# An expert ring of six split pairs and five raw tiles, with one-hots, splits and low parts moved

## The chip, the cores and the metric

The kernel runs on one core of a Trainium2 chip. A core has a matrix engine (TensorE; PE in the profile, its weight loads PEld), a vector engine (VectorE, DVE), a scalar engine (ScalarE, ACT), GpSimd (POOL) and a queue engine that only issues transfers (SyncE, SP). Each runs its own instructions in order and waits on semaphores for the others. Tiles live in SBUF (128 partitions); results of PE land in PSUM. The metric is the device time of one execution in microseconds, the median over runs.

## The reference

A two-layer encoder over 512 tokens of width 1024. Each layer has a mixer (differential attention in layer 0, a sparse latent attention in layer 1), attention to a memory of 256 tokens, and a hierarchical mixture of 16 experts, each followed by a residual and a layer norm. The change touches the mixture:

```python
g_sel = argmax(t @ w_group + b_group)                # 4 groups of 4 experts
top_val, top_idx = top_k(e_logits of the group, 2)   # two experts for each token
top_w = softmax(top_val) * g_gate
for e in range(16):
    hid = silu(t @ w_gate[e]) * (t @ w_up[e])        # 1024 -> 512
    y = y + combine[:, e:e+1] * (hid @ w_down[e])    # 512 -> 1024
```

All in float32. An expert's weights are three matrices of 2 MB, 6 MB together.

## The kernel before

**Split matmuls.** A product in float32 is made of three in the faster format fp32r: an operand is split into a high part (ACT copies it to fp32r, L208 for weights, L258 for activations) and a low part (DVE subtracts the high part from the raw tile, L209 and L259), and PE adds high x high, high x low and low x high.

**Units and the ring.** An expert's weights come in six units of 1 MB, 128 x 2048: j = 0, 1 (gate), 2, 3 (up), 4, 5 (down). `Stream` (object `U`) loads a unit into a raw tile (`ahead`, on SP's queue, L233), and `get` splits it into a pair of tiles (`wsplit`). The order of all 96 units of a layer is `ORDER`: for expert p the four units into the hidden layer, then the two down units of expert p-1. There are RING = 7 split pairs, from the pools `act8` (8 tiles) and `w8` (6 tiles), and RB = 3 raw tiles. `refill(n)` makes units up to n + RING: a unit's pair is free when the unit seven back has been used. Three units are split ahead of the mixture, beside the projection in front of it (NFIRST).

**Blocks.** Tokens are gathered by expert. A block is up to 128 tokens of one expert; the experts at places p = 5 and 11 (`DBL`) have a second block (v = 16, 17). For a block, `slot_rows` makes four one-hot tiles on DVE (L833 to L843, tiles pw, pv, pb, oh), `slot_sums` multiplies them on PE (L849, pi), `slot_out` makes the row numbers sx and gate weights sw (DVE, L855 and L857), and `gather` fetches the rows with an indirect DMA from POOL's queue (L870) into a tile that POOL has set to zero (L866). For experts 0 and 1, `slot_tokens` makes the row numbers in a shorter way, from one-hots in two buffers. `turn` transposes a block on PE (L877, xgT) and splits it (xh on ACT, xl on DVE).

**The loop.** For each p, in program order, which is the order on every engine here: set the tile of a later block (p+2) to zero, its one-hots on DVE; where that expert has two blocks, also their sums on PE and their gathers; `refill` of the unit left over from the round before (`late`); gate (PE, pg, then SiLU on ACT, L1071), up (pu), each unit followed by a `refill`; sums and gather of block p+2 where it is single; the product hid (DVE, L1081); `turn` of the next block, in two halves: its transposes, then the `refill` of the up projection's last unit, then xh and xl; the down projection of p-1 (py, L918, scaled on ACT, L907, and added to memory by an indirect DMA from POOL's queue, L908); transposes and split of hid (hT, hsh, hsl). At p = 0 the slots of experts 0 and 1 are computed after `turn`. The router (`router`) is a generator whose parts are issued in places: position numbers, permutation (`prm`), weights (`who, cv`), and the list of extra blocks (`xtra`, at p = 2), whose count is loaded into registers at p = 4 for a conditional part at the end.

PSUM tiles of 1024 columns (`sc2`: xgT and py among them) have two buffers, so py for an expert, or a second transpose, waits until xl has read an earlier xgT.

Of the kernel before, what the change touches and what calls it, by code (L numbers as in the profile page):

```python
# [22 lines left out]
P = 128  # L23
# [41 lines left out]
def encoder(ctx: ExitStack, tc: tile.TileContext, I, out):  # L65
# [137 lines left out]

    def wsplit(raw, hi, lo, scale=None, chunks=1):
        if scale is None:
            n = raw.shape[1] // chunks
            for c in (slice(j * n, j * n + n) for j in range(chunks)):
                nc.scalar.activation(hi[:, c], raw[:, c], AF.Copy)  # L208
                nc.vector.tensor_tensor(lo[:, c], raw[:, c], hi[:, c].bitcast(F32), op=ALU.subtract)  # L209
        else:  # L210
            for k in range(raw.shape[1]):
                nc.scalar.activation(hi[:, k], raw[:, k], AF.Copy, scale=scale(k))
                nc.vector.scalar_tensor_tensor(lo[:, k], raw[:, k], scale(k), hi[:, k].bitcast(F32),
                                               op0=ALU.mult, op1=ALU.subtract)
        return hi, lo

    class Stream:
# [4 lines left out]

        def add(self, name, src, shape=(P, 8, 256), scale=None, alloc=w8, depth=RB):
            loads = src if callable(src) else (lambda raw: [(raw, src)])
            self.units.append((name, loads, list(shape), scale, alloc, depth))

        def ahead(self, depth, q=nc.sync):
            for m in range(self.n, min(self.n + depth, len(self.units))):
                if m not in self.raw:
                    nm, loads, shape, _, alloc, _ = self.units[m]  # L230
                    self.raw[m] = r8(f"{nm}r", shape)
                    for sl, src in loads(self.raw[m]):
                        q.dma_start(sl, src)  # L233

        def get(self, name, chunks=1):
            n = self.n
            nm, _, shape, scale, alloc, depth = self.units[n]
            assert nm == name, (nm, name)
            self.ahead(1)
            W = wsplit(self.raw[n], alloc(name + "h", shape), alloc(name + "l", shape), scale, chunks)  # L240
            self.n += 1
            self.ahead(depth)
            return W

# [572 lines left out]
    def slot_tokens(pos, nm):  # L817
        o = tp(f"pi{nm}")
        for t in range(NT):
            oh = sb.tile([P, P], F16, tag="oh", name=f"oh{nm}{t}", bufs=2)  # L820
            nc.vector.tensor_scalar(oh, iota16, pos[:, t:t + 1], None, op0=ALU.is_equal)
            nc.tensor.matmul(o[:, 0:1], oh, tokm[:, t:t + 1], start=t == 0, stop=t == NT - 1)
        idx = small(f"ix{nm}", [P, 1], I32)
        last_ix[0] = nc.vector.tensor_scalar(idx, o[:, 0:1], float(NONE), None, op0=ALU.add)
        return idx

    def slot_rows(who, cv, e, base, nm):

        pw = small(f"pw{nm}", [P, NT, 8], bufs=3)
        pv = small(f"pv{nm}", [P, NT, 8], bufs=2)  # L830
# [7 lines left out]
        for t in range(NT):  # L838
            oh.append(sb.tile([P, P], BF16, tag="ohf", name=f"oh{nm}{t}", bufs=4))
            if base is None:  # L840
                nc.vector.tensor_scalar(oh[t], iotab, pw[:, t, 0:1], None, op0=ALU.is_equal)  # L841
            else:
                nc.vector.tensor_scalar(oh[t], iotab, base, pw[:, t, 0:1], op0=ALU.add, op1=ALU.is_equal)  # L843
# [86 lines left out]
    ORDER = moe_order()  # L930

    PERM, XU = {}, {}

    def moe(i, R, before, after, first):
# [12 lines left out]
        def block(j):  # L947
# [13 lines left out]
            def W(q):  # L961
                src, shape = us[q]
                hi, lo, raw = [t.rearrange("p (a b) -> p a b", a=shape[1]) for t in X + [XR]]
                nc.sync.dma_start(raw, src)
# [80 lines left out]
        with tc.manual_schedule(engines={ENG.PE, ENG.Activation, ENG.DVE}):  # L1045
            for v in range(S0):
                gather(slot_tokens(posm[:, :, v], name(v)), xg[v])
                if v == 0:
                    refill(3 - RING)
            refill(5 - RING)  # L1050
            turn(0)()
            prm, PERM[i] = next(rt)
            who, cv = next(rt)
            refill(6 - RING)
            late = None
            for p in range(NE):
                cur, nxt = blocks[p], blocks.get(p + 1, [])
                new = blocks.get(p + 2, [])
                for v in new:
                    xg[v] = gather_begin(name(v))  # L1060
                    R_[v] = rows(v)
                    if len(new) > 1:
                        SX[v] = slot_out(R_[v], slot_sums(R_[v], name(v)), name(v))
                        gather(SX[v][0], xg[v])
                if late is not None:
                    refill(late)
                refill(way_in(pg, cur, p, 0))
                n = way_in(pg, cur, p, 1)
# [8 lines left out]
                n = way_in(pu, cur, p, 3)  # L1077
                if len(new) == 1:
                    pt = slot_sums(R_[new[0]], name(new[0]))
                for v in cur:  # L1080
                    nc.vector.tensor_tensor(hid[v], hid[v], pu.pop(v), op=ALU.mult)  # L1081
# [33 lines left out]
            for n in range(2):  # L1115
                down_part(1, py, hT, W[1], (n,))
            X = [w8(f"X{i}{k}", [P, 2048]) for k in range(2)]
            XR = act8(f"XR{i}", [P, 2048], F32)
            XG = gather_begin(f"{i}_x")
# [259 lines left out]
    def plan():  # L1379
# [43 lines left out]
        for i in range(2):  # L1423
# [110 lines left out]
```

## Time and profile before

| | |
|---|---|
| median of 3 runs | 1908.26 us (1907.23 to 1912.56) |
| the profiled execution | 1901.26 us, of it the span 1899.5 us |
| mean granted clock of PE | 0.916 |
| PE busy | 1603.6 us (84%) |
| DVE busy | 1195.4 us (63%) |
| ACT busy | 853.3 us (45%) |
| POOL busy | 259.5 us (14%) |

The span is the time from the first to the last instruction that the profile shows. A row of the table of stages gives a stretch, its length, then for each engine its busy time and number of instructions, then the granted clock (1.00 is full), the mean busy share of the 16 DMA engines and what they moved in GB/s. A row of waits gives who waited for what: the total in us, how often, the longest. A row of a timeline gives start, duration, engine, line, operation, the tile written and those read, shapes, a count, and in brackets the idle time of the engine before it and what ended that. Expert loops run from about 567 to 991 us (layer 0) and from 1454 to 1875 us (layer 1).

### The profile page before, as it was taken

Reading aid. Unit: us, or ns where it says so; the run is one execution under the profiler, and the core shown is the slowest. Engines: PE = TensorE matmul, PEld = TensorE weight load, DVE = VectorE, ACT = ScalarE, POOL = GpSimd, SP = SyncE. Lnnn points to the kernel's source line nnn. Section 1 sums busy time; section 2 is a strip of 40 time slices with the busy share of each in tenths; the row PEclk is TensorE's granted clock in tenths of the full one; section 3 lists DMA queues with packets and bytes.
Section 4 is the critical chain, followed back from the end, with each engine's and each line's share of the span. In section 5 each row is a group of like instructions: output and inputs, shape, how many; then the busy total and the mean of one; then the engine's idle time right before and its main releaser. Section 6 shows DMA issues by size and latency. Waiting matters only on the chain. (4 is left out here: it accounts for less than half of the span.)

```text
span 1899.5 us, 24536 instructions
## 1 busy us (share of the span) xinstructions
PE 1603.6 (84%) x9244; PEld 1354.6 (71%) x9244; DVE 1195.4 (63%) x2317; ACT 853.3 (45%) x1142; POOL 259.5 (14%) x230
## 2 busy tenths in 40 slices
PE   7999899988957688879887889999895768868895
PEld 7887798887855577767667656898694657757773
DVE  4444546453477776777657698463358786678675
ACT  4343436232324465655543445533323555556562
POOL 1000001110040221222210000020012121232111
PEclk9999999899977799989897999999997879989998
DMA  7220325233165787887774102141516777788784
GB/s 202 67 67 1 101 95 192 92 123 113 67 234 174 236 276 236 267 270 242 252 246 142 45 23 78 54 144 51 164 47 210 253 239 239 243 271 276 239 285 135
DMA packets 122435, 317.67 MB, mean 167 GB/s; under 512 B 23773, under 2 KB 81117, under 8 KB 97728
## 3 DMA queue, kind: packets, MB, share of 16 engines
q1 hardware_dynamic: 104496, 272.00, 43.0%
q0 software_dynamic: 17808, 43.96, 7.6%
q8 instruction: 77, 1.26, 0.3%
q14 instruction: 54, 0.44, 0.1%
HBM read 299.38 MB, written 36.70 MB: 177 GB/s over the span
## 5 line engine op out<-in xcount | busy, mean ns | idle before, releaser
L870 POOL DMA_INDIRECT xg<-h_d,sx x32 | 57.7, 1804 | 422.0 <-DVE sx L857 357.9
L908 POOL DMA_INDIRECT acc_d<-y,sx x34 | 78.1, 2297 | 241.5 <-ACT y L907 211.8
L208 ACT ACTIVATE mw_1h<-mw_1r 128x2048 fp32r<-128x2048 f32 x32 | 61.4, 1917 | 108.9 <-PE pg L891 76.2
L209 DVE TENSOR_TENSOR mw_3l<-mw_3r,mw_3h 128x2048 fp32r<-128x2048 f32 x32 | 73.3, 2289 | 49.3 <-ACT mw_3h L208 49.3
L209 DVE TENSOR_TENSOR mw_2l<-mw_2r,mw_2h 128x2048 fp32r<-128x2048 f32 x32 | 73.3, 2291 | 44.1 <-ACT mw_2h L208 43.2
L209 DVE TENSOR_TENSOR mw_5l<-mw_5r,mw_5h 128x2048 fp32r<-128x2048 f32 x32 | 73.3, 2290 | 43.9 <-ACT mw_5h L208 43.6
L209 DVE TENSOR_TENSOR mw_1l<-mw_1r,mw_1h 128x2048 fp32r<-128x2048 f32 x32 | 73.3, 2289 | 35.6 <-ACT mw_1h L208 34.8
L208 ACT ACTIVATE mw_5h<-mw_5r 128x2048 fp32r<-128x2048 f32 x32 | 61.2, 1914 | 63.9 <-PE py L918 35.8
L208 ACT ACTIVATE mw_3h<-mw_3r 128x2048 fp32r<-128x2048 f32 x32 | 61.3, 1916 | 61.9 <-DMA mw_3r<-in_moe_w_up_dram 40.3
L918 PE MATMUL py<-mw_4h,hsh 128*128 128x512 f32 x144 | 63.3, 439 | 24.4 <-DVE xl L259 23.0
L209 DVE TENSOR_TENSOR mw_4l<-mw_4r,mw_4h 128x2048 fp32r<-128x2048 f32 x32 | 73.4, 2294 | 16.0 <-ACT mw_4h L208 14.9
L849 PE MATMUL pi<-pb,oh 128*128 128x6 bf16 x144 | 14.4, 175 | 81.1 <-DVE oh L841 68.8
L208 ACT ACTIVATE mw_4h<-mw_4r 128x2048 fp32r<-128x2048 f32 x32 | 61.3, 1916 | 48.0 <-DMA mw_4r<-in_moe_w_down_dram 27.9
L891 PE MATMUL pg<-mw_0h,xl 128*128 128x512 f32 x144 | 66.5, 462 | 10.4 <-DVE xl L259 10.3
L209 DVE TENSOR_TENSOR mw_0l<-mw_0r,mw_0h 128x2048 fp32r<-128x2048 f32 x32 | 73.1, 2284 | 1.7 <-ACT mw_0h L208 1.4
L849 PEld LDWEIGHTS <-oh 128*128 128x128 bf16 x144 | 8.8, 99 | 91.5 <-DVE oh L841 70.1
L891 PE MATMUL pg<-mw_0h,xh 128*128 128x512 f32 x144 | 70.0, 486 | 3.4 <-ACT xh L258 3.4
L208 ACT ACTIVATE mw_2h<-mw_2r 128x2048 fp32r<-128x2048 f32 x32 | 61.2, 1913 | 22.5 <-DMA mw_2r<-in_moe_w_up_dram 22.4
L877 PE MATMUL xgT<-ident,xg 128*128 128x128 f32 x288 | 45.3, 306 | 29.9 <-DVE xl L259 20.2
L891 PE MATMUL pg<-mw_0l,xh 128*128 128x512 f32 x144 | 65.8, 457 | 0.0
L208 ACT ACTIVATE mw_0h<-mw_0r 128x2048 fp32r<-128x2048 f32 x32 | 61.4, 1918 | 8.5 <-DMA mw_0r<-in_moe_w_gate_dram 8.5
L877 PEld LDWEIGHTS xgT<-ident,xg 128*128 128x128 f32 x288 | 38.8, 197 | 32.2 <-DVE xl L259 21.9
(944 smaller groups left out, 5653.2 us busy)
## 6 DMA issues: line engine op xcount, KB each, us to landing
mw_0r<-in_moe_w_gate_dram SPq DMA_DIRECT2D x32, 1024.0 KB, 5.5
mw_1r<-in_moe_w_gate_dram SPq DMA_DIRECT2D x32, 1024.0 KB, 6.6
mw_2r<-in_moe_w_up_dram SPq DMA_DIRECT2D x32, 1024.0 KB, 6.3
mw_3r<-in_moe_w_up_dram SPq DMA_DIRECT2D x32, 1024.0 KB, 5.9
mw_4r<-in_moe_w_down_dram SPq DMA_DIRECT2D x32, 1024.0 KB, 5.5
mw_5r<-in_moe_w_down_dram SPq DMA_DIRECT2D x32, 1024.0 KB, 5.5
mhx<-acc_d POOLq DMA_DIRECT2D x8, 512.0 KB, 6.8
x<-in_x_dram SPq DMA_DIRECT2D x4, 512.0 KB, 6.7
```

The costliest lines, as they stand in the source:

```text
L208: nc.scalar.activation(hi[:, c], raw[:, c], AF.Copy)
L209: nc.vector.tensor_tensor(lo[:, c], raw[:, c], hi[:, c].bitcast(F32), op=ALU.subtract)
L849: nc.tensor.matmul(o[:, 0:6], rows[2][t], rows[1][:, t, :], start=t == 0, stop=t == NT - 1)
L870: nc.gpsimd.indirect_dma_start(out=x, out_offset=None, in_=h_d[:, :], in_offset=bass.IndirectOffsetOnAxis(ap=idx[:, 0:1], axis=0), bounds_ ...
L877: nc.tensor.transpose(pt[:, ts(k)], x.rearrange("n (p k) -> n k p", k=8)[:, k, :], ident)
L891: nc.tensor.matmul(o, xT[l][:, a, :], W[r][:, k, :], start=a == j == 0, stop=a == 7 and j == 2)
L908: nc.gpsimd.indirect_dma_start(out=acc_d[:, :], out_offset=bass.IndirectOffsetOnAxis(ap=ix[:, 0:1], axis=0), in_=y, in_offset=None, bounds ...
L918: nc.tensor.matmul(o, hs[a][:, ts(2 * q + f)], Dq[b][:, f, c], start=q == f == k == 0, stop=q == f == 1 and k == 2)
```

## The change

- **Ring.** RING goes from 7 to 6 split pairs, and raw tiles from three to RAWS = 5. Both are now fixed tiles, kept in `Cells` for each layer: unit n uses pair n mod 6 and raw tile n mod 5; the two added raw tiles come from the pool of the pair that was given up. NFIRST goes from 3 to 2. The tiles of the conditional part at the end are taken from these cells.
- **Low parts on Pool.** `wsplit` and `get` take an engine. For the last unit of an expert (j = 5), except expert 0, the low part is a subtraction on POOL's queue.
- **One-hots lead.** In each round the one-hots of all new blocks, at p = 0 and 1 also those of block p itself, are issued first; their sums come after the up projection, and sx, sw and the gathers after hid, also for doubled experts. One-hot tiles have 8 buffers, shared with those of `slot_tokens`; `pw` has two instead of three. Single blocks compare a float16 iota plus a constant.
- **xl ahead.** `turn` of the next block is issued whole, ahead of the `refill` of the up projection's last unit.
- **Router and start.** `prm` is issued ahead of the first `turn`; refills at the start are fewer and later; `xtra` moves from p = 2 to p = 5, the load of its count from p = 4 to p = 12.

```diff
-NFIRST = 3
-RING = 7
+NFIRST = 2
+RING = 6
+RAWS = 5
...
-                nc.vector.tensor_tensor(lo[:, c], raw[:, c], hi[:, c].bitcast(F32), op=ALU.subtract)
+                eng.tensor_tensor(lo[:, c], raw[:, c], hi[:, c].bitcast(F32), op=ALU.subtract)
...
-            oh.append(sb.tile([P, P], BF16, tag="ohf", name=f"oh{nm}{t}", bufs=4))
+            oh.append(sb.tile([P, P], BF16, tag="ohf", name=f"oh{nm}{t}", bufs=8))
             if base is None:
-                nc.vector.tensor_scalar(oh[t], iotab, pw[:, t, 0:1], None, op0=ALU.is_equal)
+                nc.vector.tensor_scalar(oh[t], iota16, BIG, pw[:, t, 0:1], op0=ALU.add, op1=ALU.is_equal)
...
+    class Cells:
+        def raw(self, n):
+            def get(name, shape):
+                q = n % RAWS
+                if q < RB:
+                    t = self.tile(("r", q), lambda nm, sh, dt: r8(nm, sh), F32)
+                else:
+                    t = self.tile(("r", q), act8, F32)
+                return self.view(t, shape)
+            return get
+
+        def part(self, n):
+            k = iter("hl")
+            def get(name, shape):
+                q = n % RING
+                return self.view(self.tile((next(k), q), w8 if 1 <= q <= 3 else act8, F32R), shape)
+            return get
...
-                unit[made[0]] = U.get(f"mw{i}_{p}_{j}")
+                unit[made[0]] = U.get(f"mw{i}_{p}_{j}", eng=nc.gpsimd if j == 5 and p else nc.vector)
...
                 gather(slot_tokens(posm[:, :, v], name(v)), xg[v])
-                if v == 0:
-                    refill(3 - RING)
-            refill(5 - RING)
+                refill(2 + v - RING)
+            prm, PERM[i] = next(rt)
             turn(0)()
-            prm, PERM[i] = next(rt)
             who, cv = next(rt)
-            refill(6 - RING)
-            late = None
+            late = 5 - RING
             for p in range(NE):
                 ...
                 for v in new:
                     xg[v] = gather_begin(name(v))
+                if p < S0:
+                    new = new + [p]
+                for v in new:
                     R_[v] = rows(v)
-                    if len(new) > 1:
-                        SX[v] = slot_out(R_[v], slot_sums(R_[v], name(v)), name(v))
-                        gather(SX[v][0], xg[v])
                 ...
-                if len(new) == 1:
-                    pt = slot_sums(R_[new[0]], name(new[0]))
+                pts = {v: slot_sums(R_[v], name(v)) for v in new}
                 for v in cur:
                     nc.vector.tensor_tensor(hid[v], hid[v], pu.pop(v), op=ALU.mult)
                     xT.pop(v)
-                if len(new) == 1:
-                    v = new[0]
-                    SX[v] = slot_out(R_[v], pt, name(v))
-                    gather(SX[v][0], xg[v])
+                for v in new:
+                    SX[v] = slot_out(R_[v], pts.pop(v), name(v))
+                    if v != p:
+                        gather(SX[v][0], xg[v])
                 for v in nxt[:1]:
-                    done = turn(v)
-                    refill(n)
-                    done()
-                if p == 0:
-                    for v in range(S0):
-                        R_[v] = rows(v)
-                        SX[v] = slot_out(R_[v], slot_sums(R_[v], name(v)), name(v))
-                if p == 2:
-                    xtra = next(rt)
+                    turn(v)()
+                refill(n)
                 ...
+                if p == 5:
+                    xtra = next(rt)
                 if p + 3 == NE:
                     sel, wsel = last_select()
-                if p == 4:
+                if p == 12:
                     nx = nc.values_load(xtra["n"][0:1, 0:1], engines=IF_ENG, min_val=0, max_val=NX)
...
-                free = ORDER.index((S0, 0)) if n < RING else len(ORDER)
+                free = ORDER.index((S0, 0)) if n < 4 else len(ORDER)
                 U.add(f"mw{i}_{p}_{j}", loads, (P, 4, 512) if j < 4 else (P, 2, 1024),
-                      alloc=(act8, w8)[n % 7 % 2], depth=min(RB, free - n - 1))
+                      alloc=CELLS[i].part(n), raw=CELLS[i].raw(n), depth=min(RAWS, free - n - 1))
```

More of the change, by code (lines that the diff above doesn't have):

```diff
@@ L202, in rsqrt, with wsplit @@
         return y
-    def wsplit(raw, hi, lo, scale=None, chunks=1):
+    def wsplit(raw, hi, lo, scale=None, chunks=1, eng=nc.vector):
         if scale is None:
@@ L221, in __init__, with add @@
             self.units, self.raw, self.n = [], {}, 0
-        def add(self, name, src, shape=(P, 8, 256), scale=None, alloc=w8, depth=RB):
+        def add(self, name, src, shape=(P, 8, 256), scale=None, alloc=w8, depth=RB, raw=r8):
             loads = src if callable(src) else (lambda raw: [(raw, src)])
-            self.units.append((name, loads, list(shape), scale, alloc, depth))
+            self.units.append((name, loads, list(shape), scale, alloc, depth, raw))
         def ahead(self, depth, q=nc.sync):
@@ L229, in ahead, with get @@
                 if m not in self.raw:
-                    nm, loads, shape, _, alloc, _ = self.units[m]
-                    self.raw[m] = r8(f"{nm}r", shape)
+                    nm, loads, shape, _, _, _, raw = self.units[m]
+                    self.raw[m] = raw(f"{nm}r", shape)
                     for sl, src in loads(self.raw[m]):
                         q.dma_start(sl, src)
-        def get(self, name, chunks=1):
+        def get(self, name, chunks=1, eng=nc.vector):
             n = self.n
-            nm, _, shape, scale, alloc, depth = self.units[n]
+            nm, _, shape, scale, alloc, depth, _ = self.units[n]
             assert nm == name, (nm, name)
             self.ahead(1)
-            W = wsplit(self.raw[n], alloc(name + "h", shape), alloc(name + "l", shape), scale, chunks)
+            W = wsplit(self.raw[n], alloc(name + "h", shape), alloc(name + "l", shape), scale, chunks, eng)
             self.n += 1
@@ L819, in slot_tokens @@
         for t in range(NT):
-            oh = sb.tile([P, P], F16, tag="oh", name=f"oh{nm}{t}", bufs=2)
+            oh = sb.tile([P, P], F16, tag="ohf", name=f"oh{nm}{t}", bufs=8)
             nc.vector.tensor_scalar(oh, iota16, pos[:, t:t + 1], None, op0=ALU.is_equal)
@@ L827, in slot_rows @@
     def slot_rows(who, cv, e, base, nm):
-        pw = small(f"pw{nm}", [P, NT, 8], bufs=3)
+        pw = small(f"pw{nm}", [P, NT, 8], bufs=2)
         pv = small(f"pv{nm}", [P, NT, 8], bufs=2)
@@ L930, in encoder, with __init__, tile, view @@
     ORDER = moe_order()
+    class Cells:
+        def __init__(self, i):
+            self.i, self.t = i, {}
+        def tile(self, key, alloc, dtype):
+            if key not in self.t:
+                self.t[key] = alloc(f"cell{self.i}_{'_'.join(map(str, key))}", [P, 2048], dtype)
+            return self.t[key]
+        def view(self, t, shape):
+            return t.rearrange("p (a b) -> p a b", a=shape[1])
+        def raw(self, n):
[13 more added lines that the diff above has]
+            return get
+    CELLS = {i: Cells(i) for i in range(2)}
     PERM, XU = {}, {}
@@ L962, in W @@
                 src, shape = us[q]
-                hi, lo, raw = [t.rearrange("p (a b) -> p a b", a=shape[1]) for t in X + [XR]]
+                hi, lo, raw = [t.rearrange("p (a b) -> p a b", a=shape[1]) for t in X]
                 nc.sync.dma_start(raw, src)
@@ L1060, in moe @@
                     xg[v] = gather_begin(name(v))
+                if p < S0:
+                    new = new + [p]
+                for v in new:
                     R_[v] = rows(v)
-                    if len(new) > 1:
-                        SX[v] = slot_out(R_[v], slot_sums(R_[v], name(v)), name(v))
-                        gather(SX[v][0], xg[v])
                 if late is not None:
                     refill(late)
+                    late = None
                 refill(way_in(pg, cur, p, 0))
@@ L1116, in moe @@
                 down_part(1, py, hT, W[1], (n,))
-            X = [w8(f"X{i}{k}", [P, 2048]) for k in range(2)]
-            XR = act8(f"XR{i}", [P, 2048], F32)
+            X = [CELLS[i].t[key] for key in (("h", 0), ("l", 0), ("r", 0))]
             XG = gather_begin(f"{i}_x")
```

## The prediction

> **What bounds the kernel now.** I read the page first (its span), then the busy time of stages cut at the first `pg` matmul of each expert, then the waits of PE in the expert loop, then the timelines of DVE, POOL and PE around the longest waits.
>
> ```profile
> span 1899.5 us, 24536 instructions
> ```
> ```profile
> core 0: us, PE busy (x) PEld busy (x) DVE busy (x) ACT busy (x) POOL busy (x), PEclk, DMA share, GB/s
> 567.10:598.60 31.50, 17.23 (x73) 13.17 (x73) 26.54 (x84) 12.31 (x10) 1.96 (x2) 0.72 0.57 201
> 598.60:701.50 102.90, 80.40 (x367) 65.70 (x365) 79.32 (x113) 56.23 (x40) 21.63 (x13) 0.86 0.73 238
> 701.50:731.30 29.80, 29.80 (x143) 24.77 (x141) 19.05 (x21) 15.12 (x12) 3.11 (x3) 0.98 0.67 217
> 731.30:763.00 31.70, 26.16 (x114) 21.04 (x114) 18.92 (x21) 15.51 (x13) 7.09 (x4) 0.89 0.71 237
> 763.00:860.50 97.50, 78.98 (x368) 64.39 (x366) 76.26 (x86) 58.57 (x42) 26.38 (x16) 0.91 0.86 278
> 860.50:890.90 30.40, 30.40 (x142) 25.18 (x141) 18.97 (x21) 15.04 (x12) 3.09 (x3) 0.96 0.69 223
> 890.90:923.30 32.40, 26.44 (x116) 21.32 (x114) 18.97 (x21) 15.51 (x13) 6.52 (x4) 0.89 0.70 237
> 923.30:941.40 18.10, 18.10 (x90) 14.92 (x89) 12.86 (x17) 12.17 (x10) 4.31 (x3) 1.00 0.86 265
> 941.40:963.00 21.60, 19.77 (x86) 16.01 (x85) 17.42 (x15) 15.29 (x11) 3.25 (x2) 0.92 0.88 301
> 963.00:991.00 28.00, 23.63 (x102) 18.20 (x101) 10.64 (x8) 9.03 (x9) 7.04 (x5) 1.00 0.63 189
> 834.80:860.50 25.70, 20.23 (x99) 16.83 (x98) 20.77 (x20) 15.85 (x13) 8.04 (x4) 0.91 0.89 291
> 1454.00:1875.00 421.00, 349.31 (x1576) 283.81 (x1576) 298.75 (x403) 224.48 (x164) 84.96 (x52) 0.90 0.74 243
> ```
> The first ten rows are layer 0's experts p=0, 1 to 4, 5, 6, 7 to 10, 11, 12, 13, 14 and 15, 423.9 us together; then p=10 by itself, then layer 1's loop, 421.0 us. p=5 and 11 hold two token blocks. In p=13 PE never stops: 18.1 us at clock 1.00 is what PE asks for one expert. The nine single experts (1 to 4, 7 to 10, 13) took 102.9 + 97.5 + 18.1 = 218.5 us, 24.3 each. No engine is full: PE idles while DVE waits or works at something else. The waits of PE in layer 0's loop name what is late:
>
> ```profile
> PE pi L849 <- DVE oh L841: 34.8, 4, 13.1
> PE py L918 <- DVE xl L259: 11.5, 2, 6.0
> PE xgT L877 <- DVE xl L259: 10.3, 2, 5.5
> PE pg L891 <- DVE xl L259: 4.9, 3, 1.8
> ```
> One-hots cost 34.8 us a layer, late `xl` 26.7. The same instructions one after another:
>
> ```profile
> 568.25 0.16 DVE L712 TENSOR_SCALAR rt<-ct 128x16 f32<-128x16 f32 x1
> 572.53 0.17 DVE L735 CAST rt<-rt 128x16 int32<-128x16 f32 x1
> 576.75 2.28 DVE L209 TENSOR_TENSOR mw_2l<-mw_2r,mw_2h 128x2048 fp32r<-128x2048 f32 x1
> 641.50 0.22 DVE L768 TENSOR_SCALAR rt<-iota,rt 128x16 f32<-128x16 f32 x1
> 647.92 2.29 DVE L209 TENSOR_TENSOR mw_5l<-mw_5r,mw_5h 128x2048 fp32r<-128x2048 f32 x1
> 651.82 0.78 PE L849 MATMUL pi<-pb,oh 128*128 128x6 bf16 x4 [13.07 <-DVE oh L841]
> ```
> The first three are the start, used below. The router's part for extra blocks (641.50 to 647.92, 6.4 us, issued at p=2) stands on DVE ahead of a low part and of the one-hots, for which PE stands 13.07 us before expert 3.
>
> **The change part by part.** I price a single expert's round on DVE from start-to-start times:
>
> ```profile
> 764.51 0.69 DVE L259 TENSOR_TENSOR hsl<-hT,hsh 128x512 fp32r<-128x512 f32 x1 [3.37 <-ACT hsh L258]
> 765.12 0.24 DVE L833 SCALAR_TENSOR_TENSOR pw<-rt,rt,rt 128x32 f32<-128x32 f32 x1
> 766.66 2.29 DVE L209 TENSOR_TENSOR mw_0l<-mw_0r,mw_0h 128x2048 fp32r<-128x2048 f32 x1
> 768.87 2.28 DVE L209 TENSOR_TENSOR mw_1l<-mw_1r,mw_1h 128x2048 fp32r<-128x2048 f32 x1
> 778.64 0.68 DVE L1081 TENSOR_TENSOR hid<-hid,pu 128x512 f32<-128x512 f32 x1
> 779.24 0.16 DVE L855 TENSOR_REDUCE sw<-pi 128x2 f32<-128x6 f32 x1
> L259 DVE TENSOR_TENSOR xl<-xgT,xh x18: 1210/1218/1225, 567.1 to 963.7; 128x1024 fp32r<-128x1024 f32 x18
> ```
> hsl 0.61 (764.51 to 765.12), a block's slot rows with one-hots 1.54 (to 766.66), a low part 2.21, the product 0.60, sw and sx 0.35, xl 1.2. With six low parts 17.6 us, with five 15.3.
>
> *Low parts of unit (p,5) on Pool, p over 0.* 15 a layer leave DVE. No row has a Pool subtraction of 2048 columns; the nearest are these.
>
> ```profile
> L318 POOL TENSOR_TENSOR xp0x<-xp0x,b x4: 721/729/764, 526.5 to 548.1; 128x256 f32<-128x256 f32 x4
> 371.76 1.72 POOL L317 TENSOR_SCALAR op0x<-op0x,rsyop0ln 128x256 f32<-128x256 f32 x1 [45.47 <-DVE rsyop0ln L201]
> 390.60 0.87 POOL L318 TENSOR_TENSOR op0x<-op0x,b 128x256 f32<-128x256 f32 x1
> 390.80 1.76 DVE L308 SCALAR_TENSOR_TENSOR op0x<-op0x,op0ln3m,g 128x1024 f32<-128x1024 f32 x1
> 373.26 1.27 DVE L308 SCALAR_TENSOR_TENSOR op0x<-op0x,op0ln1m,g 128x1024 f32<-128x1024 f32 x1
> ```
> Eight times 0.72 is 5.8 us, the upper end; DVE's own 2.29 the lower, since Pool needs 0.72 for 256 columns where DVE needs 0.69 for 512. I take 5.3: the same operation an eighth as wide is the nearest row, less a little for a start that does not grow. The other cost is in the last two rows: DVE's L308 takes 1.27, but 1.76 when Pool's tensor-tensor began 0.2 us ahead of it. Two-operand work of both engines excludes itself, so the moved part still takes DVE's time: bounds 0 (DVE idle meanwhile) and the whole 5.3. Taking the whole, DVE's round is 15.3 + 5.3 = 20.6 us, dearer than today's 17.6. The Trainium skill (SBUF — State Buffer, Who interferes with whom) says that a VectorE instruction with two SBUF inputs and a GpSimd instruction that reads SBUF fully block each other; the trace agrees, by that 1.76. The skill's GPSIMD Engine Reference (3.1 Elementwise) gives 4.497 us for this add at 2048 columns; by it the round would be 15.3 + 4.5 = 19.8, and the sum would go by DMA's price below, as good as unchanged. On Pool's queue the low part stands behind the scatter and the memset and ahead of the next gather; PE needs it some 15 us into the expert, so it is covered unless it takes over 11 us. Behind a double expert it waits for the second scatter:
>
> ```profile
> POOL acc_d L908 <- DMA acc_d<-y,sx: 15.2, 2, 8.0
> ```
> 8 us later, ending as PE arrives: 0 to 4 us each time, I take 2, twice a layer.
>
> *Six pairs, five raw tiles.* The price of a hi part, and SP's waits for raw tiles:
>
> ```profile
> L208 ACT ACTIVATE mw_1h<-mw_1r 128x2048 fp32r<-128x2048 f32 x32 | 61.4, 1917 | 108.9 <-PE pg L891 76.2
> SPq L233 <- DVE mw_0l L209: 77.6, 14, 8.9
> SPq L233 <- DVE mw_3l L209: 40.3, 14, 4.2
> ```
> The waits are the first and last of six such rows (326.5 us together). With five raw tiles two more 1 MB loads are on their way, so DMA no longer runs dry while one unit is split. Its price per expert: layer 1's loop moved 243 GB/s for 421.0 us, 6.39 MB for each of 16; at the 291 GB/s of p=10 that is 22.0 us, at a share of 1.00 instead of 0.89, 19.6. Middle 20.8. One pair less: a unit is split when the unit six back is used up, five units (5 x 3.0 us of PE, a sixth of 18.1 each) before its use, against 1.9 for hi and 2.3 for lo: covered; without that cover each unit would cost PE up to 4.2 us.
>
> So a single expert costs the largest of PE 18.1, DVE with Pool 20.6 and DMA 20.8: I take 21.0. The ends: 19.6, DMA full and Pool's part hidden, and 23, the upper Pool part (15.3 + 5.8 = 21.1) or the slower DMA (22.0) with a microsecond or two of waits in order.
>
> *One-hots ahead.* Those of the next blocks are still first in DVE's round, but for two blocks PE's sums and the gathers come after the up-projection, not at the top of p=3 and p=9. DVE then has the time of 48 of a round's 72 large matmuls, some 11 of PE's 18.1 us, to make them: the stop goes. What is late next is DVE's product and xl, within the 21. The router's 6.4 us move to p=5, behind which PE has p=6's 26 us. Gathers of doubled blocks start 11 us later, a round ahead of need. Loading the block count moves to p=12, and the buffers of `pw` (3 to 2) and of one-hots (to 8) change no wait that I can find: 0.
>
> *xl ahead of its split.* One low part and its ACT and DMA waits no longer stand before xl: the 26.7 us of PE's waits on it go; SP's load of that unit is not delayed by xl, 1.2 us, as that raw tile is one of five.
>
> *Start, p=0.* The permutation part of the router now comes ahead of xl(0), while DVE waits for the gather; its 4.3 us (568.25 to 572.53) leave the round. DVE's router end 576.75 becomes 572.5; then 2 x 1.54 rows, 5 x 2.21 low parts, 0.60, 2 x 0.35, 1.2: 589.1, when expert 1 can start, against 598.6. p=0 goes from 31.5 to 22.0. Two units split ahead instead of three cost nothing, with DVE idle for the gather.
>
> **Sum, layer 0.** 22.0 (p=0) + 84 (1 to 4) + 29.8 + 27 (p=6, PE 26.2) + 84 + 30.4 + 27 + 21 + 21.6 + 28 = 374.8, plus 4 for Pool behind doubles, 379 against 424: 45 us. Layer 1's loop is 3 us shorter now: 43. From the profiled execution's 1901.3 us (span 1899.5 and 1.8 around it) 88 go: 1813. The median of the runs, 1908.3, lies 7.0 above that execution: 1820; I say 1822.
>
> **The rivals.** *PE and DMA alone bound (14%)*: Pool's part falls into DVE's idle time and DMA fills its share: 19.6 a single, 18 singles x 1.4 = 25 us less, 1797. For it: DVE is idle 3.4 us at 764.51; against: it leaves DMA no gap. *DVE with Pool, or DMA, binds harder (26%)*: in-order waits on raw tiles and on the exclusion add up, 23 a single, 36 us more, 1858. For it: a share of 0.89 is the most a stage shows; against: it was reached with three raw tiles. *The waits move (6%)*: one-hot waits come back as waits for `hid` or xl, as DVE's queue feeds all three; only the 4.3 us at each start stay: 1899. Against it: DVE is busy 76.26 of 97.5. *Pool too slow (8%, the other side)*: no row has Pool write fp32r, and its tensor-scalar rows of 256 columns take up to 1.72 us, eight times which is 13.8. At 12 us DVE's round is 27.3: 18 x 6.3 = 113 us more, 1935. It decides from 88/18 = 4.9 us over 21.0, a Pool part of 10.6 us, nearly twice the upper end.
>
> **How the numbers follow.** Forecast 46%, 1805 to 1845 by itself. From 1788 to 1880 lie it, most of the first rival and most of the second: about 0.8. Within 0.3% (5.7 us, about what a measurement here can tell from no change) lies part of the waits that move: 0.05. Faster 0.87, slower 0.08.
>
> **What would show it.** Right: no wait of `pi` on one-hots over 2 us, waits on xl near zero, p=1 to 4 near 84 us, DMA share over 0.9 in singles, Pool's low part at 4 to 6 us with DVE low parts beside it stretched above 2.3. Wrong: Pool's part over 10 us, `py` waiting on it, SP waiting on Pool for a raw tile while DMA idles, or long waits of `hT` on `hid`.

## The result and the profile after

The changed kernel takes 1802.88 us (median of four runs, 1802.31 to 1806.42) against 1908.21 us before: a ratio of 0.9448, interval 0.9429 to 0.9467. That is 105 us less; the forecast was 1822 (1788 to 1880). The direction and the range held, but the term of DMA did not: it was put as high as DVE's round with Pool's low part, so that Pool's part looked free. The experiments below show that this part costs 55 us: without it the same kernel takes 1747.8 us.

Two lines of the changed kernel's page, its span and the engines' busy time:

```profile
span 1800.5 us, 24571 instructions
PE 1597.6 (89%) x9244; PEld 1345.9 (75%) x9244; DVE 1229.5 (68%) x2287; ACT 851.8 (47%) x1142; POOL 379.0 (21%) x260
```

PE's share rises from 84% to 89% because the span fell; POOL's busy time rises by 120 us. The stages of the changed kernel, cut like those of before (layer 0's experts p=0, 1 to 4, 5, 6, 7, 8 to 10, 11, 12, 13, 14, 15; then layer 0's loop and layer 1's). Columns as before: stretch and length, busy time of PE, its weight loads, DVE, ACT, POOL, then granted clock, DMA share, GB/s.

```profile
568.70:589.30 20.60, 16.02 (x68) 12.50 (x69) 19.62 (x51) 14.14 (x11) 0.00 (x0) 0.83 0.45 158
589.30:670.10 80.80, 76.22 (x371) 61.77 (x369) 79.28 (x93) 55.68 (x40) 33.04 (x18) 0.99 0.91 322
670.10:701.00 30.90, 30.90 (x143) 25.59 (x142) 21.91 (x22) 15.29 (x12) 8.79 (x4) 0.94 0.73 252
701.00:734.20 33.20, 28.75 (x115) 22.93 (x114) 26.60 (x48) 15.33 (x13) 10.16 (x5) 0.85 0.72 238
734.20:752.40 18.20, 18.20 (x90) 14.67 (x90) 14.33 (x16) 12.18 (x9) 7.09 (x3) 1.00 0.47 118
752.40:819.10 66.70, 60.07 (x280) 47.60 (x278) 65.16 (x66) 46.29 (x33) 31.94 (x16) 0.97 0.95 348
819.10:849.40 30.30, 29.61 (x143) 24.30 (x142) 21.79 (x22) 15.25 (x12) 8.83 (x4) 1.00 0.77 265
849.40:877.00 27.60, 25.43 (x115) 20.46 (x114) 21.54 (x20) 15.36 (x13) 10.14 (x5) 0.94 0.87 296
877.00:895.30 18.30, 18.30 (x92) 14.80 (x90) 14.47 (x16) 12.24 (x9) 7.98 (x4) 1.00 0.41 111
895.30:915.70 20.40, 18.26 (x86) 14.69 (x86) 19.39 (x14) 14.98 (x11) 9.53 (x4) 1.00 1.00 390
915.70:943.60 27.90, 26.30 (x103) 20.50 (x101) 11.31 (x7) 10.43 (x9) 15.54 (x7) 0.88 0.62 191
568.70:943.60 374.90, 348.06 (x1576) 279.83 (x1576) 315.39 (x367) 227.17 (x165) 143.03 (x66) 0.95 0.78 272
1404.30:1775.30 371.00, 342.93 (x1576) 276.02 (x1576) 315.48 (x368) 227.34 (x165) 146.00 (x66) 0.97 0.78 270
```

All of the gain lies in the two loops: 423.9 to 374.9 and 421.0 to 371.0 us, 99 us, as much as the span fell. Experts 1 to 4 went from 102.9 to 80.8, and DVE is busy for 79.28 of those 80.8, its stops beside Pool included: taken together, DVE sets these stages. One by one, by the starts of their first gate matmuls, they took 19.2, 17.9, 20.5 and 23.2 us; the first two are as fast as in the run without Pool's parts below (19.2 and 17.9), the last two are not (18.1 and 19.3 there). p=6 did not gain at all (31.7 before, 33.2 now).

What PE waits for in the changed kernel (the waits of the whole run, both layers; the prediction's rows were of one layer):

```profile
PE pi L850 <- DVE oh L842: 12.9, 9, 2.7
PE hT L897 <- DVE sw L856: 10.1, 4, 4.5
PE py L919 <- DVE xl L260: 9.3, 4, 3.1
PE xgT L878 <- DVE xl L260: 7.5, 4, 1.9
PE hT L897 <- DVE hid L1113: 6.2, 5, 2.0
PE pg L892 <- DVE xl L260: 3.7, 10, 0.7
```

The one-hot waits fell from 34.8 us in one layer to 12.9 in two, with 2.7 the longest instead of 13.1. The groups that hold the new price, with Pool's low parts first (count, then busy time and mean ns of one):

```profile
L210 POOL TENSOR_TENSOR cell_l<-cell_r,cell_h 128x2048 fp32r<-128x2048 f32 x30 | 151.8, 5059 | 19.7 <-ACT cell_h L209 19.7
L210 DVE TENSOR_TENSOR cell_l<-cell_r,cell_h 128x2048 fp32r<-128x2048 f32 x162 | 386.2, 2417 | 61.1 <-ACT cell_h L209 60.8
L837 DVE CAST pb<-pw 128x24 bf16<-128x24 f32 x36 | 62.7, 1741 | 1.2
```

Pool's part takes 5.06 us. The third row is the surprise: a cast of 24 columns that takes 0.18 us when undisturbed takes 1.74 on average (0.52 in the kernel before). The timeline of POOL and DVE in one expert shows why:

```profile
759.79 1.53 POOL L867 MEMSET xg<- 128x1024 f32 x1
760.71 5.15 POOL L210 TENSOR_TENSOR cell_l<-cell_r,cell_h 128x2048 fp32r<-128x2048 f32 x1
759.85 0.19 DVE L836 TENSOR_TENSOR pw<-pw,pv 128x32 f32<-128x32 f32 x1
760.07 5.83 DVE L837 CAST pb<-pw 128x24 bf16<-128x24 f32 x1
765.82 0.73 DVE L842 TENSOR_SCALAR oh<-iota,pw 128x128 bf16<-128x128 f16 x4
```

The cast begins 0.3 us after Pool's memset and ends at 765.90, 0.04 us after Pool's low part (765.86). For 5.6 us DVE does nothing, at the head of its round, with one-hots, five low parts and xl queued behind. Elsewhere it is the first slot-row instruction that waits, likewise until Pool's end:

```profile
780.02 5.20 POOL L210 TENSOR_TENSOR cell_l<-cell_r,cell_h 128x2048 fp32r<-128x2048 f32 x1
780.06 5.23 DVE L834 SCALAR_TENSOR_TENSOR pw<-rt,rt,rt 128x32 f32<-128x32 f32 x1
```

### The profile page after: what moved, and what is told of

Its sections match the earlier page's. It is cut to its first block, busy times and chain, and to the rows that moved or that the text cites. A ratio compares the mean times of both kernels' runs of the same rounds, so it can differ in the third digit from the quotient of the medians.

```text
span 1800.5 us, 24571 instructions
## 1 busy us (share of the span) xinstructions
PE 1597.6 (89%) x9244; PEld 1345.9 (75%) x9244; DVE 1229.5 (68%) x2287; ACT 851.8 (47%) x1142; POOL 379.0 (21%) x260
## 5 line engine op out<-in xcount | busy, mean ns | idle before, releaser
L209 ACT ACTIVATE cell_h<-cell_r 128x2048 fp32r<-128x2048 f32 x192 | 364.9, 1915 | 136.9 <-PE py L919 32.4
L210 DVE TENSOR_TENSOR cell_l<-cell_r,cell_h 128x2048 fp32r<-128x2048 f32 x162 | 386.2, 2417 | 61.1 <-ACT cell_h L209 60.8
L210 POOL TENSOR_TENSOR cell_l<-cell_r,cell_h 128x2048 fp32r<-128x2048 f32 x30 | 151.8, 5059 | 19.7 <-ACT cell_h L209 19.7
L919 PE MATMUL py<-cell_h,hsh 128*128 128x512 f32 x288 | 121.6, 422 | 10.7 <-DVE xl L260 9.3
L892 PE MATMUL pg<-cell_h,xh 128*128 128x512 f32 x288 | 120.2, 417 | 2.2 <-ACT xh L259 2.2
L892 PE MATMUL pg<-cell_h,xl 128*128 128x512 f32 x288 | 118.0, 410 | 3.8 <-DVE xl L260 3.7
L919 PE MATMUL py<-cell_h,hsl 128*128 128x512 f32 x288 | 117.9, 409 | 0.3 <-DVE hsl L260 0.3
L919 PE MATMUL py<-cell_l,hsh 128*128 128x512 f32 x288 | 117.9, 409 | 0.0
L892 PE MATMUL pg<-cell_l,xh 128*128 128x512 f32 x288 | 116.7, 405 | 0.0
L892 PE MATMUL pu<-cell_l,xh 128*128 128x512 f32 x288 | 112.0, 389 | 0.0
L892 PEld LDWEIGHTS pg<-cell_h,xl 128*128 128x128 f32 x288 | 56.5, 196 | 23.1 <-DVE xl L260 11.1
L919 PEld LDWEIGHTS py<-cell_l,hsh 128*128 128x128 f32 x288 | 57.7, 200 | 12.3 <-POOL cell_l L210 0.8
```

The costliest lines, as they stand in the source:

```text
L210: eng.tensor_tensor(lo[:, c], raw[:, c], hi[:, c].bitcast(F32), op=ALU.subtract)
L892: nc.tensor.matmul(o, xT[l][:, a, :], W[r][:, k, :], start=a == j == 0, stop=a == 7 and j == 2)
L919: nc.tensor.matmul(o, hs[a][:, ts(2 * q + f)], Dq[b][:, f, c], start=q == f == k == 0, stop=q == f == 1 and k == 2)
```

## The experiments

The change has three parts that can be put in and out: the order on the engines, the raw tiles, Pool's low parts. In one table, all with six pairs but the first row (the kernel before, seven pairs); ratios are to the kernel before on the same chip, with their intervals:

| order | raw tiles | j=5 on | us | ratio |
|---|---|---|---|---|
| old, 7 pairs | 3 | DVE | 1908 to 1913 | 1 |
| old | 3 | DVE | 1912.5 | 1.0011 (1.0000 to 1.0022) |
| new | 3 | DVE | 1863.3 | 0.9745 (0.9719 to 0.9771) |
| new | 3 | Pool | 1911.7 | 0.9997 (0.9978 to 1.0016) |
| old | 5 | DVE | 1809.8 | 0.9461 (0.9434 to 0.9487) |
| old | 5 | Pool | 1859.6 | 0.9728 (0.9704 to 0.9751) |
| new | 5 | Pool (the change) | 1802.9 | 0.9448 (0.9429 to 0.9467) |
| new | 5 | DVE | 1747.8 | 0.9150 (0.9127 to 0.9173) |

Read in pairs: the new order is worth 49 to 62 us, two more raw tiles 103 to 116 us, and Pool's low parts cost 48 to 55 us, nearly whatever the other two are. (The ratios, which allow for runs on different chips, give the same within 4 us. The old order with three raw tiles and Pool was not run.)

### All low parts on DVE

```diff
-unit[made[0]] = U.get(f"mw{i}_{p}_{j}", eng=nc.gpsimd if j == 5 and p else nc.vector)
+unit[made[0]] = U.get(f"mw{i}_{p}_{j}")
```

> The changed kernel with every low part on DVE; ring, raw tiles and order stay. Theory A (Pool's low part takes DVE's time whole): in the changed kernel DVE's stretched rows cost 2.5 us for each Pool part (162 low parts at 2417 ns instead of 2290, 36 casts at 1741 ns instead of 178: 21 + 56 us for 30 parts), against 2.29 us moved, so DVE's busy time in a layer's loop stays near 315 us, SP's 94 us of waits on Pool's low parts go, and the time is 1795 to 1806. Rival B (Pool relieves DVE): 2.2 us come back to each single expert that DVE sets, 18 of them or more: 1835 or above.

1747.76 us, 55.1 less than the changed kernel. Both expectations were wrong: A had the right cause and put 47 us too little on it. Its stages (p=0; 1 to 4; 6; 7 to 10; 13; 14; layer 0's loop):

```profile
568.40:589.10 20.70, 16.13 (x69) 12.65 (x69) 19.72 (x51) 14.20 (x11) 0.00 (x0) 0.83 0.44 150
589.10:663.60 74.50, 74.35 (x371) 61.27 (x369) 72.92 (x96) 55.29 (x39) 18.67 (x14) 0.98 0.96 347
693.90:724.70 30.80, 25.36 (x115) 20.51 (x114) 24.21 (x49) 15.32 (x13) 5.56 (x4) 0.89 0.73 256
724.70:797.90 73.20, 73.04 (x366) 60.48 (x366) 70.58 (x85) 57.36 (x41) 19.24 (x14) 1.00 0.97 342
851.90:869.80 17.90, 17.90 (x90) 14.87 (x89) 15.72 (x19) 14.15 (x11) 4.05 (x3) 1.00 0.91 296
869.80:887.60 17.80, 17.80 (x87) 14.91 (x86) 16.84 (x15) 14.29 (x11) 1.91 (x1) 1.00 1.00 365
568.40:914.00 345.60, 330.94 (x1576) 271.07 (x1576) 291.97 (x382) 227.38 (x166) 69.86 (x51) 0.98 0.84 295
```

PE is busy in 74.35 of 74.50 us: the singles run at PE's own pace. Although DVE does 15 low parts more in the loop (15 x 2.29 = 34.3 us), it is busy 23.4 us less (291.97 against 315.39). So Pool's parts stretched DVE's rows by 57.7 us, 3.8 us each: three quarters of the 5.06 for which Pool ran. My count ahead of the run took only the low parts and casts and missed the slot rows.

DVE's stops are not the whole price that PE pays. Layer 0's loop is 29.3 us shorter here. PE stands still 12.2 us less (14.7 us against 26.8), and the same 1576 matmuls keep it busy 17.1 us less (330.94 against 348.06). The granted clock is 0.98 instead of 0.95; my estimate from these figures is that the clock makes about 12 of the 29 us (0.05 x 374.9 less 0.02 x 345.6). Some of PE's stops in the change have a stretch at half clock behind them, as the rows of p=6 further down show. No run changes the clock by itself, so that the stops lower it is not shown.

### Three raw tiles, with Pool and without

```diff
-RAWS = 5
+RAWS = 3
```

> The changed kernel with three raw tiles instead of five. Theory A (DMA runs dry while a unit is split unless more loads are on their way): share of DMA in the singles falls from 0.91 to 0.95 back below 0.87, a single expert takes 22 to 24 us instead of 20.2 to 22.2, time 1835 to 1875. Rival B (the order of DVE alone sets the loads free early enough): within 5 us of the changed kernel, 1798 to 1808.

1911.7 us: back at the kernel before, 37 us beyond theory A's upper end. B falls; A's direction holds, its size does not.

The same with every low part on DVE:

> The new order alone: three raw tiles and every low part on DVE, six pairs. Theory A (raw tiles worth 30 to 70 us, Pool's part nothing): the same as three raw tiles with Pool, 1835 to 1875, within 6 us of that run. Rival B (Pool's low part frees a raw tile late, and with three raw tiles that hurts, so without it the order alone is enough): 1800 to 1815.

1863.3 us, in A's range, but 48 us below the run with Pool, not within 6 of it: here too Pool's parts are a price. What the loads wait for shows in the turn of a raw tile. One turn in the kernel before, from its timelines (load issued, high part, low part, next load into the same tile):

```profile
802.60 0.34 SPq L233 DMA_DIRECT2D mw_0r<-in_moe_w_gate_dram  x1
807.82 1.91 ACT L208 ACTIVATE mw_0h<-mw_0r 128x2048 fp32r<-128x2048 f32 x1 [0.27 <-DMA mw_0r<-in_moe_w_gate_dram]
816.17 2.29 DVE L209 TENSOR_TENSOR mw_0l<-mw_0r,mw_0h 128x2048 fp32r<-128x2048 f32 x1
818.50 0.33 SPq L233 DMA_DIRECT2D mw_3r<-in_moe_w_up_dram  x1
```

Landing 5.2 us, high part 1.9, a wait of 6.4 for DVE (which makes one-hots), low part 2.3; the next load goes out 0.04 us after the low part ends. The wait is a long one, behind a doubled expert's one-hots; the mean is 1.05. Means over 24 units of layer 0 (the 13th to the 36th), from the starts and ends of these four instructions of each unit, in us:

| kernel | tiles | load to high | high | to low | low | turn | turn / tiles | a unit took |
|---|---|---|---|---|---|---|---|---|
| before | 3 | 8.50 | 1.92 | 1.05 | 2.29 | 13.76 | 4.6 | 4.68 |
| new order, DVE | 3 | 6.81 | 1.92 | 0.71 | 2.29 | 11.73 | 3.9 | 3.95 |
| the change | 5 | 9.81 | 1.91 | 3.26 | 2.74 | 17.73 | 3.5 | 3.55 |
| new order, DVE | 5 | 10.49 | 1.92 | 1.71 | 2.28 | 16.40 | 3.3 | 3.29 |

The last two columns agree because a raw tile is loaded again 0.03 us after its low part in all four kernels, with five tiles too: loads come at the turn divided by the tiles. That agreement alone does not say that the tiles set the pace; the times do, 1863.3 us with three tiles and 1747.8 with five in the same order. PE asks for a unit in 3.0 us (17.9 / 6) in a single expert. So three tiles would need a turn of 9 us, and five may take 15 us before a single is late; with five, a load waits longer for its high part (10.49 us) without holding PE up as much.

### Four raw tiles

```diff
-RAWS = 5
+RAWS = 4
```
(with every low part on DVE)

> As e1_no_pool with four raw tiles instead of five. In the traces a raw tile is never free for more than 0.03 us, and its turn from load to load is 11.7 us with three (e4_order_only: 6.8 to hi, 1.9 hi, 0.7 wait, 2.3 low part). Theory A (loads come at the turn divided by the tiles: 3.9 us a unit with three, where PE asks for 3.0): with four 11.7 to 12.5 / 4 = 2.9 to 3.1 us, all but PE's rate: 1748 to 1770. Rival B (each raw tile more brings DMA the same gain, 116 us for two): 1795 to 1815.

1774.2 us, ratio 0.9285 (0.9265 to 0.9304): the first tile brings about 89 us of the 116, the second 26. That is A's curve and not B's straight line, but 4 us over A's end, since the turn did not stay: 13.99 us (8.90 from load to high part, where three tiles had 6.81), 3.5 a unit.

### The old order, with Pool and without

```diff
-            prm, PERM[i] = next(rt)
             turn(0)()
+            prm, PERM[i] = next(rt)
             who, cv = next(rt)
-            late = 5 - RING
+            refill(5 - RING)
+            late = None
...
-                if p < S0:
-                    new = new + [p]
                 for v in new:
                     R_[v] = rows(v)
+                    if p + 2 in DBL:
+                        SX[v] = slot_out(R_[v], slot_sums(R_[v], name(v)), name(v))
+                        gather(SX[v][0], xg[v])
+                if p + 2 in DBL:
+                    new = []
...
-                    if v != p:
-                        gather(SX[v][0], xg[v])
+                    gather(SX[v][0], xg[v])
                 for v in nxt[:1]:
-                    turn(v)()
-                refill(n)
+                    done = turn(v)
+                    refill(n)
+                    done()
+                if p == 0:
+                    for v in range(S0):
+                        R_[v] = rows(v)
+                        SX[v] = slot_out(R_[v], slot_sums(R_[v], name(v)), name(v))
...
-                if p == 5:
+                if p == 2:
                     xtra = next(rt)
```

> The changed kernel with the order of the kernel before: router's permutation part after xl(0), slot rows of the first two blocks behind xl(1), one-hots, sums and gathers of a doubled expert's blocks at the top of the round, a low part between the transposes and xl, the extra blocks' router part at p=2. Six pairs, five raw tiles and Pool's low parts stay. Theory A (PE's waits on one-hots and xl were a cost of their own, 34.8 and 26.7 us a layer, and 4.3 at the start): most of it comes back, 1870 to 1905. Rival B (they were only where a late load showed, so five raw tiles remove them too): 1815 to 1840.

1859.6 us, 57 over the change: 10 below A's range, 20 above B's. PE again stops for one-hots (67.7 us in both layers, 12.4 the longest). Its waits for xl are 32.5 us in both layers, 3.9 the longest, where the kernel before had 26.7 in one layer, 6.0 the longest.

The same with every low part on DVE:

> The order of the kernel before (as in e3_old_order) with every low part on DVE; six pairs and five raw tiles stay. Theory A (the order's gain is its own: PE's stops for one-hots at p=0, 2 and 8 and for xl): 1795 to 1812, as much over e1_no_pool as e3_old_order was over the changed kernel (57 us). Rival B (the old order was only dear because Pool kept DVE from making the one-hots): 1760 to 1780.

1809.8 us, 62.1 over the same kernel with the new order: A. The order is worth its own time, whether Pool takes part or not.

### Two pieces of the order by themselves

Both with every low part on DVE and five raw tiles. First, one unit's split between the transposes and xl:

```diff
-                    turn(v)()
-                refill(n)
+                    done = turn(v)
+                    refill(n)
+                    done()
```

> Every low part on DVE (as in e1_no_pool, 1747.8 us), and one unit is split between the transposes and xl, as in the kernel before. Theory A (the wait for xl was a cost of its own, 26.7 us a layer in the kernel before): 20 us or more over e1_no_pool, 1768 or above. Rival B (it was where a late load showed; with five raw tiles the low part ahead of xl is ready, 2.3 us, and PE has the down projection in between): 1748 to 1758.

1774.7 us, 27.0 more: A, at its lower end. The time is lost in few experts: p=1 took 23.5 us instead of 19.2, p=4 23.1 instead of 19.3, p=10 23.2 instead of 19.2 (starts of the first gate matmuls). Next, the slots of doubled experts at the top of the round:

```diff
                 for v in new:
                     R_[v] = rows(v)
+                    if p + 2 in DBL:
+                        SX[v] = slot_out(R_[v], slot_sums(R_[v], name(v)), name(v))
+                        gather(SX[v][0], xg[v])
+                if p + 2 in DBL:
+                    new = []
```

> As e1_no_pool, but the one-hots, sums and gathers of a doubled expert's two blocks are at the top of p=3 and p=9 again, where PE needs them at once. Theory A (PE stops for as long as DVE's queue holds work ahead of them): the 4.6 to 10 us that e8_old_order_no_pool showed there, four times, 18 to 34 us: 1766 to 1782. Rival B (those stops came from the router's part at p=2 alone): 1748 to 1758.

1783.2 us, 35.4 more: A, 1 us over its end. PE's four stops for these one-hots are 19.6 us of it; the rest is not taken apart. The two pieces together make 62.4, all that the old order cost in the run above, although that also had the old start and the router's part at p=2. So the pieces do not add up: p=0 is 10 us longer there (30.6 against 20.7), and other waits are shorter behind it.

### The ring of six

Six pairs with the old order, three raw tiles and every low part on DVE. It is made from the changed kernel by the edits above, so the smaller pieces of the change stay in it: fixed tiles, two units split ahead, other one-hot buffers, the count loaded at p=12.

> The kernel before with a ring of six pairs instead of seven: old order, three raw tiles, every low part on DVE. Theory A (a pair comes free 15 us of PE's work before its next use, so the seventh pair does nothing): within 6 us of the kernel before, 1902 to 1916. Rival B (the seventh pair was used to work ahead beside doubled experts): 1920 to 1950.

1912.5 us, the same as before: A. The pair that was given up did nothing there; a seventh pair beside five raw tiles was not tried.

### What it is about Pool's part that costs

Two kernels with every low part on DVE, where Pool gets work whose result nobody uses, ahead of 13 memsets a layer:

```diff
-    def gather_begin(nm):
+    def gather_begin(nm, side=False):
         x = t4("a", f"xg{nm}")
+        if side:
+            one = ident.unsqueeze(1).to_broadcast([P, 8, P])
+            for k in range(2):
+                nc.gpsimd.tensor_tensor(x.rearrange("p (a b) -> p a b", a=8), one, one, op=ALU.subtract)
         nc.gpsimd.memset(x, 0.0)
...
-                    xg[v] = gather_begin(name(v))
+                    xg[v] = gather_begin(name(v), side=p > 0 and v == new[0])
```

> Every low part on DVE (as in e1_no_pool, 1747.8 us), and Pool does work that nobody waits for: ahead of 13 of a layer's 15 memsets of a gather buffer in p over 0, two subtractions of 1024 columns with two SBUF inputs into that buffer. Theory A (the price of Pool's low part is that DVE stands still while Pool's subtraction runs): the 55.0 us between the changed kernel and e1_no_pool are 1.8 us a part, 26 parts are 48 us: 1785 to 1800, and DVE rows beside the subtractions stretch by 4 us. Rival B (the price is that the low part comes late, 5.1 us instead of 2.3 and behind the scatter, and holds its raw tile): within 6 us of e1_no_pool, 1742 to 1754.

1815.4 us, 67.6 more than without: A, and 15 us beyond its range. The range took the net price of a part in the change, where 2.3 us come off DVE for each; here nothing comes off. That this makes the 15 us is argued, not shown. The price does not need a low part that comes late: here no low part is on Pool. POOL's and DVE's timelines:

```profile
609.02 4.96 POOL L870 TENSOR_TENSOR xg<-ident 128x1024 f32<-128x1024 f32 x2
614.04 0.95 POOL L871 MEMSET xg<- 128x1024 f32 x1
610.77 1.28 DVE L834 SCALAR_TENSOR_TENSOR pw<-rt,rt,rt 128x32 f32<-128x32 f32 x1
612.25 1.78 DVE L836 TENSOR_TENSOR pw<-pw,pv 128x32 f32<-128x32 f32 x1
614.06 0.96 DVE L837 CAST pb<-pw 128x24 bf16<-128x24 f32 x1
```

Two 32-column instructions wait out one subtraction each (1.28 and 1.78 instead of 0.24 and 0.19), the cast the memset.

> As e5_pool_beside, but Pool's extra work is three memsets of 1024 columns (about 4.5 us), which read nothing. Theory A (two instructions that both read SBUF exclude each other): 1742 to 1756, no stretch of DVE's low parts. Rival C (Pool's time as such counts, because gathers and scatters stand behind it on its queue): the same time as e5_pool_beside.

Its edit is three `nc.gpsimd.memset(x, 0.0)` in place of the two subtractions. 1754.7 us, 6.9 more: A, and C falls. Its timelines in the same expert:

```profile
610.58 3.59 POOL L869 MEMSET xg<- 128x1024 f32 x3
610.16 0.24 DVE L834 SCALAR_TENSOR_TENSOR pw<-rt,rt,rt 128x32 f32<-128x32 f32 x1
610.83 1.32 DVE L837 CAST pb<-pw 128x24 bf16<-128x24 f32 x1
```

Memsets do not touch DVE's low parts (2285 ns on average in this run, 2285 without them), but the cast waits for one (1.32 us instead of 0.18), and the one-hots behind it grow from 485 to 593 ns on average. The Trainium skill (SBUF — State Buffer, Who interferes with whom) says that casts can run in a mode that uses the port pair shared with GpSimd, and that whoever issues second is blocked entirely. These rows agree, by the 1.32 us. The cast of the change shown above (760.07) began ahead of Pool's subtraction (760.71), behind a memset, and was held to the end of both; the longest of the change's 36 casts took 5.90 us.

### A version that beats both

```diff
-                if p < S0:
-                    new = new + [p]
+                if 0 < p <= S0:
+                    new = new + [p - 1]
...
-                    if v != p:
+                    if v >= p:
                         gather(SX[v][0], xg[v])
...
-                if p == 5:
+                if p == 4:
                     xtra = next(rt)
```
(with every low part on DVE)

> Every low part on DVE, the extra blocks' router part at the end of p=4 instead of p=5, so that DVE does it beside the doubled expert 5, and the slot rows of blocks 0 and 1 a round later (p=1 and 2 instead of 0 and 1). Theory A (what is left of PE's waits in e1_no_pool is DVE's work at the wrong place: 5.4 us at p=6 and 4.5 us at p=0, each layer): the first goes, the second falls by one block's rows and sums, 1.9 us: 1730 to 1738. Rival B (granted clock or DMA sets p=6, whose clock was 0.89): 1742 to 1748.

1734.7 us, ratio 0.9066 (0.9038 to 0.9094): A. Its stage p=6:

```profile
693.50:717.20 23.70, 23.70 (x115) 19.34 (x114) 19.32 (x21) 15.36 (x13) 5.59 (x4) 1.00 0.96 335
```

23.7 us with PE never idle, against 30.8 with the router's part a round later, and the granted clock is 1.00 (0.89 there).

## Why the prediction was right or wrong

The direction, the range and the total of the sum held: layer 0's loop took 374.9 us where the sum said 379, layer 1's 371.0 where it said 378. Part of that is luck: p=6 took 6 us more than its term, while experts 1 to 4, p=13 and the 4 us for Pool behind doubles were charged 10 us too much together. By its steps:

**Pool's low part: the size and the lock were right; the lock was charged whole, 5.3 us, and DVE lost 3.8.** The part took 5.06 us. DVE's round with Pool was put at 20.6 us; in experts 1 to 4 DVE was busy 19.8 us each (79.28 / 4), and they took 20.2. The nine singles took 80.8 + 18.2 + 66.7 + 18.3 = 184.0 us, 20.4 each, against 21.0. The one L308 row (1.27 us, 1.76 beside Pool) named the mechanism for instructions with two operands. What was overlooked is that others are held too: casts, and the router's tensor-scalar in p=6. The kernel before already shows it, inside the 6.4 us that were read as the router's part: at 643.21 a copy of two columns takes 2.01 us on DVE and ends 0.04 us after a memset on Pool (643.67 to 645.18).

**The term of DMA was mis-sized, and with it the verdict on Pool.** The prediction put DMA at 20.8 us an expert (19.6 to 22.0) by scaling 291 GB/s at a share of 0.89. Without Pool experts 1 to 4 and 7 to 10 take 18.6 and 18.3 us each at 347 and 342 GB/s, so DMA needs no more than that. p=14 of the change moved 390 GB/s, where the lower end, 19.6 us at a share of 1.00, amounts to 327 (291 / 0.89). The 291 was no limit of the DMA engines; three raw tiles did not ask for more. With 20.8 for DMA beside 20.6 for DVE, Pool's part looked free. In fact it was what kept the single experts above PE's pace, and the change's time 55 us above what the rest of it gives. That the sum came out right is luck: the true bound, DVE with Pool, lay next to the false one.

**Rival "PE and DMA alone bound" (1797) is nearer to the time than the forecast, but not its mechanism:** it had Pool's part fall into idle time and DMA full. The measured cause is the other way round, DVE is held and DMA has room. The other rivals did not come: Pool's part took 5.06 us of the 10.6 at which it would have decided, and one-hot waits came back as waits for hid only in small part (`hT` on sw and hid together 16.3 us in both layers, 4.7 before).

**Six pairs cost nothing: right** (the ring of six). **One-hots: right**; the remaining waits were to stay under 2 us, the longest is 2.7. (The 34.8 us left out a second row, waits on the one-hots of line 843, 6.1 us.) **xl ahead: right in the direction**, 27 us for both layers with five raw tiles where 26.7 for one layer was taken; waits on xl are 20.5 us in both layers after (the `py`, `xgT` and `pg` rows), not near zero. **Start: right**, p=0 took 20.6 against 22.0.

**The router's part at p=5: wrong.** It was said to lie behind 26 us of PE's work in p=6, 27 us in all; p=6 took 33.2. From the change's timeline of DVE in p=6:

```profile
703.32 5.92 DVE L769 TENSOR_SCALAR rt<-iota,rt 128x16 f32<-128x16 f32 x1
714.40 0.74 DVE L842 TENSOR_SCALAR oh<-iota,pw 128x128 bf16<-128x128 f16 x4
715.05 6.69 DVE L210 TENSOR_TENSOR cell_l<-cell_r,cell_h 128x2048 fp32r<-128x2048 f32 x3
722.51 1.22 DVE L260 TENSOR_TENSOR xl<-xgT,xh 128x1024 fp32r<-128x1024 f32 x1
```

The router's first instruction alone is held for 5.9 us, while a Pool part runs; one-hots come at 714.4 (PE waits 2.6 us for them), xl at 722.5. PE's second `py` needs the PSUM tile that this xl reads, so its cover ended there, not at the end of p=6. What I left out was the queue behind the moved part. With every low part on DVE, p=6 still takes 30.8; with the part also moved one round earlier, beside the doubled expert itself, it takes 23.7.

The prediction also left out what the granted clock does in p=6. PE's 26 us were its busy time at a clock of 0.89; at 1.00 it is 23.7. In the change it is 28.75, and the clock is about half behind both stops (columns as in the table of stages):

```profile
711.90:714.70 2.80, 0.23 (x1) 0.00 (x0) 2.56 (x16) 0.00 (x0) 0.00 (x0) 0.96 0.57 240
714.70:721.60 6.90, 6.89 (x24) 5.64 (x24) 6.90 (x6) 2.83 (x2) 0.00 (x0) 0.52 0.47 145
723.80:728.20 4.40, 4.40 (x12) 3.48 (x13) 2.13 (x1) 0.00 (x0) 0.61 (x1) 0.61 0.96 356
```

There a matmul of `py` starts every 0.43 us instead of every 0.23. So of the 9.5 us between 33.2 and 23.7, PE's stops are 4.5 and the slower matmuls 5; the two slow stretches account for that by themselves (0.48 x 6.9 and 0.39 x 4.4 us).

**Pool behind doubles, +4 us: not seen at the place.** p=7 took 18.2 and p=13 18.3 (21 forecast). SP did wait for Pool, as listed under what would make the prediction wrong, and DMA's share fell to 0.47 and 0.41 there; PE lived on units already split, and DMA's share is high in the next three experts (0.95) and in p=14 (1.00). The cost may have come there: p=8 to 10 took 22.2 us each (66.7 / 3) where 1 to 4 took 20.2. No run separates this from DVE's stops. The waits of SP in the whole run:

```profile
SPq L234 <- POOL cell_l L210: 188.6, 26, 15.9
```

**From the profiled execution to the median.** The 7.0 us by which the median before lay above its profiled execution were added; after, the median is 0.6 above (1802.88 against 1802.31). That is a third of the 19 us between forecast and result.

## What to carry to other kernels

A transfer rate read from a stage that is not full need not be the memory's: here it was what three buffers asked for. Measure the turn of a buffer (load, first reader, last reader, next load), and change the number of buffers. Work moved from DVE to GpSimd was not taken off DVE here, where DVE had two-operand instructions or casts to do beside it; compare the length on GpSimd, 5.06 us here, with the 2.29 saved. When a term of a sum looks free because another is just as large, check that other one on its own. And when PE stops, look at the granted clock behind the stop as well as at its length.

## What the runs showed of the hardware that was not expected

- A cast of 128x24 was held for 5.83 us behind a memset and a subtraction on Pool, and for 1.32 us by a memset alone; the low parts with two inputs were not stretched by memsets (2285 ns).
- One subtraction of 2048 columns on Pool took 5.06 us and cost DVE 3.8 us of standing still on average, more than the 2.29 that it takes on DVE.
- DMA moved 390 GB/s for 20.4 us at a share of 1.00 (p=14 of the change); the kernel before did not pass 301 in a stage of layer 0's loop.
- In p=6 of the change, the granted clock was 0.52 for 6.9 us behind a stop of PE of 2.6 us. A stop of 2.1 us at 764 has no lower clock behind it, and what sets the clock is not shown here.
